# A decoder trunk on one core: operands of the feed-forward matmuls 64 and 96 bytes further in their buffers

## The chip, the cores and the metric

The kernel runs as one program on one core of a Trainium2 chip. The metric is the device time of one execution in microseconds (us). The profile names the engines PE (TensorE, matmuls), PEld (TensorE, loading of the stationary operand), DVE (VectorE), ACT (ScalarE), POOL (GpSimd) and SP (SyncE, which issues the DMAs here).

## What is computed

Two decoder layers over 256 tokens of width 1024, in float32: a dilated-attention mixer, then a mixer of forgetting attention, each followed by a SwiGLU feed-forward layer, and a last RMS norm.

```python
def swiglu(h, w_gu, w_down):          # h: 256 x 1024, D_FF = 2816
    gu = h @ w_gu
    g, u = gu[..., :D_FF], gu[..., D_FF:]
    return (jax.nn.silu(g) * u) @ w_down

def reference(x, ...):
    h = x
    for i in range(2):
        j = i // 2
        if i % 2 == 0:
            h = h + dilated_mixer(rmsnorm(h, a_norm[j]), a_w_in[j], a_w_out[j])
        else:
            h = h + forgetting_mixer(rmsnorm(h, b_norm[j]), b_w_in[j], b_f[j], b_w_out[j])
        h = h + swiglu(rmsnorm(h, ffn_norm[i]), ffn_w_gu[i], ffn_w_down[i])
    return rmsnorm(h, final_norm)
```

## The kernel before

**Split operands.** Nearly every product is made with numbers split in two: `split` (L76) writes the high part of a tile with ACT (L80, type float32r) and the rest with DVE (L84). `mm3` (L236) makes one product out of three matmuls: stationary high by moving high (L239), stationary high by moving low, stationary low by moving high (both L244). Each matmul loads its own stationary operand first, 128 columns of it, so there is one weight load to one matmul. The moving operand has 256 or 512 columns.

**The feed-forward layer** (`ffn`, called once for each layer). The 2816 columns are cut into 22 blocks of 128 (index f). For block f, `up` multiplies the weights (stationary, tiles `wh` and `wl`) by the normed activations (moving, tile `xt`, 256 tokens): 2 x 8 products, 48 matmuls of 256 columns. SiLU and the product with the other half follow on ACT and DVE, and the result is split into the tiles `ah` and `al` (`act`, L797). After every second block comes the down-projection of a pair of blocks (index j, 11 pairs), which adds into the output for two halves of 128 tokens and four column blocks of 256. It is done with one level of Strassen's scheme in Winograd's form for half of the columns:

- `down(j, t)`: for pairs j up to 8, columns 0 to 511 only, 6 matmuls of 512 columns for each half t of the tokens: stationary `ah`/`al`, moving `wh`/`wl`.
- `down_7(j)`: seven products of 256 columns, so 21 matmuls, in place of eight. Their stationary operands are `ah`/`al` or the sums of activation blocks `sh`/`sl`, which `combine` (L752) makes; their moving operands are `wh`/`wl` or the sums of weight blocks `th`/`tl`, which `sums_of` (L119) makes.

For j from 1 to 7 the order on TensorE is `up`, `up`, `down(j, 0)`, `down(j, 1)`, `down_7(j)`: 96 matmuls of 256 columns, 12 of 512, 21 of 256, without a pause. For j = 8, only `down(8, 0)` stands between two `up`; the rest of it comes in the tail of the layer with pairs 9 and 10, which are done in full. The weights of pair 8 lie in the tiles `oth`/`otl`.

**Where the operands lie.** Every tile has a place in each partition's row of SBUF, given by a pool with one ring of buffers to a tag. The buffers of a tag have the size of the largest tile under it, and the tags follow each other. Of the built program these are the places of the operands that the text speaks of, as the byte address of the first buffer, the step to the next buffer, and the remainder of every buffer's address by 128:

| Operand | Tag | First address | Step | Remainder by 128 |
|---|---|---|---|---|
| wh, wl (weights) | wh, wl | 8544, 43360 | 8704 | 96 |
| oth, otl (weights of pair 8) | oth, otl | 115040, 123232 | - | 96 |
| xt (normed activations, high and low part in turn) | xt | 131872 | 1024 | 32 |
| sh, sl (sums of activation blocks) | v | 156512 | 2048 | 96 |
| ah, al (gated activations) | p | 185184 | 2560 | 96 |
| th, tl (sums of weight blocks) | bias | 210048 | 3072 | 0 |

Inside a buffer the matmuls start at multiples of 512 bytes, except in one product of the second mixer (272 columns), whose weights step by 1088 bytes, and in fp32 matmuls of the attention, which the change does not touch. So the remainder of a buffer is that of every operand taken from it. The two that meet on TensorE at one time are the moving operand of a matmul and the stationary operand of the matmul behind it, which is loaded meanwhile. The text writes such a pair as moving/stationary: 32/96 for `up`, 96/96 and 0/96 for the down-projection. The mixers' projections with `xt` stationary are 96/32.

Of the kernel before, what the change touches and what calls it, by code (L numbers as in the profile page):

```python
# [11 lines left out]
F32R = mybir.dt.float32r  # L12
# [5 lines left out]
P = 128  # L18
# [14 lines left out]
def trunk(ctx: ExitStack, tc: tile.TileContext, T, out):  # L33
# [4 lines left out]
    ap = ctx.enter_context(tc.tile_pool(name="ap", bufs=1))  # L38
# [5 lines left out]
    def first():  # L44

        return tc.high_priority(offset=300)

    def psum(tag):
        return ps.tile([P, 512], F32, tag=tag, name=f"ps_{tag}", bufs=2)
# [26 lines left out]
    def split(pair, view, src, early=True, after=None, hold=None):  # L76
        hi, lo = pair
        with first() if early else nullcontext():
            with behind_(hold):
                a = nc.scalar.activation(view(hi), src, AF.Copy)  # L80

            def low(after=None):
                with tc.issue_after(after.ins) if after else nullcontext():
                    return nc.vector.tensor_tensor(view(lo), src, view(hi).bitcast(F32), op=ALU.subtract)  # L84

            if isinstance(after, list):
                return after.append(low)
            return a, low(after)


    def piece(key, todo=None):
        if key[0][:2] == "dn" and key[1] == LATE - 1:
            wh, wl = (y.rearrange("p k c -> p (k c)") for y in fm_tile("ot", KT, 1))
        else:
            wh, wl = (wp.tile([P, WIDE], F32R, tag=y, name=y, bufs=4) for y in ("wh", "wl"))
        if key == GATED:
            wh, wl = (y.rearrange("p (k c) -> p k c", k=KT) for y in (wh, wl))
        if key[0][:2] == "dn" and key[1] < LATE:
            todo += sums_of(key, (wh, wl))
            return wh, wl  # L100
        for c in range(2):
            raw = wp.tile([P, 1024], F32, tag="raw", name="raw", bufs=5)
            u = slice(c * 1024, (c + 1) * 1024)
            nc.sync.dma_start(raw, T[key[0]][key[1]][:, u])
            view = lambda y, u=u: y[:, u]
            if key == GATED:
                raw = raw.rearrange("p (k c) -> p k c", c=256)
                view = lambda y, c=c: y[:, c * 4:c * 4 + 4, :256]
            cut = lambda after=None, hold=None, raw=raw, view=view: split((wh, wl), view, raw, False, after, hold)
            if todo is None:  # L110
                cut()
            else:
                todo.append(cut)
        if key == GATED:
            cut = lambda after=None, hold=None: split((wh, wl), lambda y: y[:, :, 256:], wf32, False, after, hold)
            todo.append(cut)
        return wh, wl

    def sums_of(key, w):  # L119

        if key[1] == LATE - 1:
            raw = [wp.tile([P, 1024], F32, tag="raw", name="raw", bufs=5) for _ in range(2)]
        else:
            both_f = ap.tile([P, KT * S], F32, tag=("oth", "otl")[key[1] % 2], name="rawd", bufs=1)
            raw = [both_f[:, c * 1024:(c + 1) * 1024] for c in range(2)]
        for c in range(2):
            nc.sync.dma_start(raw[c], T[key[0]][key[1]][:, c * 1024:(c + 1) * 1024])
        b11, b12, b21, b22 = (raw[f][:, c:c + S] for f in range(2) for c in (512, 768))
        sums = ap.tile([P, 768], F32, tag="pt", name="ts", bufs=3)
        t3, t2, t4 = (sums[:, i * S:(i + 1) * S] for i in range(3))  # L130
        pair = tuple(ap.tile([P, 768], F32R, tag="bias", name=f"t{y}", bufs=4) for y in "hl")
        summed[key] = pair

        def plus(o, a, b):
            nc.vector.tensor_tensor(o, a, b, op=ALU.add)

        def cut(c, after=None, hold=None):
            if c == 0:
                plus(t3, b12, b22)
                plus(b12, b11, b12)  # L140
                plus(t2, b22, b12)
                plus(t4, t2, b21)
            elif c == 2:
                return split(pair, lambda y: y, sums, False, after, hold)
            return split(w, lambda y: y[:, c * 1024:(c + 1) * 1024], raw[c], False, after, hold)

        return [lambda after=None, hold=None, c=c: cut(c, after, hold) for c in range(3)]
# [141 lines left out]
    def p_tile(n=512, dtype=F32, name="p"):  # L289
        return ap.tile([P, 640], dtype, tag="p", name=name, bufs=6)[:, :n]  # L290
# [115 lines left out]
    def square(i):  # L406
        return nc.scalar.activation(part[i].rearrange("p (j s) -> p j s", s=S), xs[i], AF.Square, scale=D ** -0.5)
# [5 lines left out]
    for k in range(KT):  # L413
# [3 lines left out]
        with first(), in_order(cut):  # L417
            if k == 0:
                a = nc.vector.tensor_scalar(hi[:, k], xk[k], g, None, op0=ALU.mult)
            else:  # L420
                a = nc.scalar.activation(hi[:, k], xk[k], AF.Copy, scale=g)
# [4 lines left out]
        if k in (1, 5, 7):  # L426
            with first(), in_order(cut):
                a = [square(i) for i in {1: (0, 1), 5: (2,), 7: (3,)}[k]][-1]
# [12 lines left out]
    with first(), in_order(cut):  # L441
        a = square(4)
# [22 lines left out]
    x = []  # L465
# [133 lines left out]
    for i, (hq, g, w) in enumerate(a_units):  # L599
# [15 lines left out]
        if i in (24, 31):  # L615
            x.append(hrow("x"))
            t = len(x) - 1
            nc.sync.dma_start(x[t], T["x"][t * P:(t + 1) * P, :])
        if w < 2:
# [26 lines left out]
            if w == 1:  # L646

                j = i + (hq == 0)
# [92 lines left out]
    def ffn(l, hs, xt, grow, mid):  # L741
        acc = {}
        acts = {}
        rows_f = {}
        combos = {}
# [6 lines left out]
        def combine(j, a):  # L752

            y = ap.tile([P, 512], F32, tag="pt", name="sa4", bufs=3)
            b = a.rearrange("p (b c) -> p b c", c=P)
            z = y.rearrange("p (b c) -> p b c", c=P)
            with first():
                nc.vector.tensor_tensor(z[:, :2], b[:, 1:2].to_broadcast([P, 2, P]), b[:, 0:4:3], op=ALU.subtract)
                nc.vector.tensor_tensor(z[:, 2], z[:, 1], b[:, 0], op=ALU.subtract)
                nc.vector.tensor_tensor(z[:, 3], b[:, 2], z[:, 2], op=ALU.add)  # L760
            combos[j] = tuple(ap.tile([P, 512], F32R, tag="v", name=f"s{x}", bufs=7) for x in "hl")
            split(combos[j], lambda y: y, y)

        def down_7(j):
# [31 lines left out]

        def act(f):  # L797
            if f % 2 == 0:
                acts[f // 2] = tuple(p_tile(512, F32R, f"a{y}") for y in "hl")
            return acts[f // 2], lambda y: y[:, (f % 2) * S:(f % 2 + 1) * S]  # L800

        def gated(g, u, shape):
            sa = ap.tile([P, 512], F32, tag="qr", name="sa", bufs=3)
            sg, a = (sa[:, i * S:(i + 1) * S].rearrange("p (a b) -> p a b", a=shape) for i in range(2))
            with first():
                nc.scalar.activation(sg, g, AF.Silu)
                nc.vector.tensor_tensor(a, u, sg, op=ALU.mult)
            return a
# [6 lines left out]
        def up_with(f, wt):  # L815
            sg = ap.tile([P, 512], F32, tag="qr", name="sa", bufs=3)[:, :S]
            a = pair_of(f // 2)[:, f % 2 * S:(f % 2 + 1) * S]
            g, u = (psum("mm")[:, :S] for _ in range(2))
            proj_feat(xt, wt, g, 0)
            with first():  # L820
                nc.scalar.activation(sg, g, AF.Silu)  # L821
            proj_feat(xt, wt, u, 1)
            with first():
                nc.vector.tensor_tensor(a, u, sg, op=ALU.mult)  # L824
            split(*act(f), a)
            if f % 2 and 1 < f // 2 < LATE:
                combine(f // 2, rows_f.pop(f // 2))
# [32 lines left out]
        pair = [psum(("o", "mm")[l]) for _ in range(2)]  # L860
# [16 lines left out]
        for f in range(2):  # L877
            for t in range(2):
                nc.tensor.transpose(tr[:, f * S + t * P:f * S + (t + 1) * P], rows[t][:, f, :], ident)
        act(0)  # L880
        split(acts[0], lambda y: y, tr)
        nc.scalar.activation(pair_of(0), tr, AF.Copy)
        combine(0, rows_f.pop(0))
        third = act(2)
        up(3)
        gu = o.rearrange("p (a c b) -> p a c b", a=2, c=2)
        a = gated(gu[:, :, 0, :], gu[:, :, 1, :], 2)
# [3 lines left out]
        split(*third, tr[:, :S])  # L891
        nc.scalar.activation(rows_f[1][:, :S], tr[:, :S], AF.Copy)
        combine(1, rows_f.pop(1))
        for f in range(2, NF):
            if f > 3:
                up(f)
            if f % 2 == 0:
                j = f // 2 - 1
# [178 lines left out]
    for i, (hq, w) in enumerate(b_units):  # L1077
# [5 lines left out]
        if w < 2:  # L1083
# [15 lines left out]
            if w == 1:  # L1099
                j = i + 1  # L1100
# [39 lines left out]
    for o, (a, b) in zip(acc, ((0, 512), (512, 256), (768, 256))):  # L1140
        s = slice(a, a + b)
# [8 lines left out]
    v = ap.tile([P, 2], F32, tag="rs", name="rs", bufs=4)  # L1150
# [10 lines left out]
    for n in range(2):  # L1161
        s = slice(n * 256, n * 256 + 256)
# [3 lines left out]
        s = slice(n * 256, 256 + n * 352)  # L1166
# [88 lines left out]
```

## Time and profile before

| | |
|---|---|
| Time, median of 3 runs | 732.5 us (732.27 to 734.28) |
| The profiled execution's own time | 732.42 us |
| Its span, first to last instruction | 730.6 us |
| Granted TensorE clock, mean | 0.997 |
| PE busy | 722.6 us, 5988 matmuls |
| PEld busy | 674.5 us, 5988 loads |
| DVE busy | 566.9 us |
| ACT busy | 416.9 us |
| DMA, share of 16 engines, queue q1 | 59.0% |

Between the span and the profiled execution's own time lie 1.8 us. The page lists groups of instructions by line; a matmul's duration there runs from its start until its last result, and neighbours overlap. What a matmul costs is the distance from its start to the next one's start, which the timeline shows.

### The profile page before, as it was taken

The page shows a single profiled execution, that of the slowest core. Times are in us where ns is not written, and L with a number is a line of the kernel's source. Part 1 is how long each engine was busy: PE and PEld are TensorE (multiplying, and loading weights), DVE is VectorE, ACT ScalarE, POOL GpSimd, SP SyncE. Part 2 cuts the span into 40 slices and gives each one's busy share as a digit, 9 for nine tenths or more (in the row PEclk, how much of TensorE's full clock was granted, in tenths as well). Part 3 has the DMA queues.
Part 4 walks back from the last instruction along what each step waited for, and adds up shares of the span by engine and source line. Part 5 has one row for each costly group of instructions (what it writes and reads, how often), then busy time and mean ns, then how long its engine had stood idle before and what let it go on. Part 6 is the DMA issues. An engine that isn't in the chain of part 4 may idle for free.

```text
span 730.6 us, 14753 instructions
## 1 busy us (share of the span) xinstructions
PE 722.6 (99%) x5988; PEld 674.5 (92%) x5988; DVE 566.9 (78%) x938; ACT 416.9 (57%) x659; POOL 83.5 (11%) x118
## 2 busy tenths in 40 slices
PE   9999999999999999999999999999999999999996
PEld 7999989999988899999999989999889999999995
DVE  6997998998996788877778484586878977777825
ACT  7646747648545656655546353587475655545621
POOL 0600206008105000000000014120010000000001
PEclk9999999999999999999999999999999999999998
DMA  9865856855864494766348442883548576534601
GB/s 335 309 203 174 225 180 187 278 198 146 269 196 159 124 334 163 255 209 210 121 130 266 141 156 88 297 267 130 172 148 342 175 239 213 182 127 146 219 1 59
DMA packets 55045, 141.97 MB, mean 194 GB/s; under 512 B 20257, under 2 KB 21441, under 8 KB 54977
## 3 DMA queue, kind: packets, MB, share of 16 engines
q1 hardware_dynamic: 54832, 140.81, 59.0%
q8 instruction: 47, 0.77, 0.4%
q10 hardware_dynamic: 144, 0.21, 0.1%
q14 instruction: 22, 0.17, 0.1%
HBM read 136.00 MB, written 1.07 MB: 188 GB/s over the span
## 4 chain that ended last, share of the span: by engine, by line
PE 96%; ACT 1%; DMA 1%; DVE 1%; issue 0%; SPq 0%; POOL 0%; POOLq 0%; DVEq 0%; ACTq 0%
PE ps_mm L244 44%; PE ps_mm L239 22%; PE ps_sc L244 7%; PE ps_o L244 6%; PE ps_sc L239 4%; PE ps_o L239 3%; PE ps_tr L244 2%; PE ps_o L350 2%; PE ps_tr L239 1%; DMA otl<-in_lead 1%; PE ps_sc L513 1%; PE ps_tr L232 1%; PE ps_tr L338 1%; PE ps_sc L1006 0%; PE ps_sc L495 0%; ACT wh L80 0%
## 5 line engine op out<-in xcount | busy, mean ns | idle before, releaser
L239 PE MATMUL ps_mm<-xt,wh 128*128 128x256 f32 x1120 | 311.5, 278 | 0.1
L244 PE MATMUL ps_mm<-xt,wl 128*128 128x256 f32 x1120 | 309.9, 277 | 0.1
L244 PE MATMUL ps_mm<-xt,wh 128*128 128x256 f32 x1120 | 309.7, 277 | 0.0
L80 ACT ACTIVATE wh<-raw 128x1024 fp32r<-128x1024 f32 x204 | 210.4, 1056 | 136.9 <-PE ps_mm L244 71.4
L84 DVE TENSOR_TENSOR wl<-raw,wh 128x1024 fp32r<-128x1024 f32 x204 | 248.5, 1242 | 28.6 <-ACT wh L80 28.6
L239 PEld LDWEIGHTS ps_mm<-xt,wh 128*128 128x128 f32 x1120 | 210.3, 188 | 3.2 <-issue 1.7
L244 PEld LDWEIGHTS ps_mm<-xt,wl 128*128 128x128 f32 x1120 | 210.6, 188 | 0.3 <-DVE wl L84 0.3
L244 PEld LDWEIGHTS ps_mm<-xt,wh 128*128 128x128 f32 x1120 | 210.4, 188 | 0.2
L824 DVE TENSOR_TENSOR a<-ps_mm,sa 128x256 f32<-128x256 f32 x38 | 16.0, 422 | 50.4 <-PE ps_mm L244 50.4
L209 POOL TENSOR_SCALAR rs<-ssq 128x1 f32<-128x1 f32 x7 | 2.7, 391 | 419.6 <-ACT junk L218 419.6
L80 ACT ACTIVATE wh<-rawd 128x1024 fp32r<-128x1024 f32 x32 | 33.6, 1056 | 28.5 <-PE ps_mm L244 22.6
L239 PE MATMUL ps_mm<-wh,xt 128*128 128x512 f32 (+1 forms) x144 | 49.8, 346 | 0.0
L244 PE MATMUL ps_mm<-wh,xt 128*128 128x512 f32 (+1 forms) x149 | 49.2, 335 | 0.0
L244 PE MATMUL ps_mm<-wl,xt 128*128 128x512 f32 (+1 forms) x149 | 49.1, 335 | 0.0
L322 POOL COPY v<-v 32x256 f32<-32x256 f32 x64 | 40.4, 631 | 69.4 <-ACT v L317 66.8
L84 DVE TENSOR_TENSOR wl<-rawd,wh 128x1024 fp32r<-128x1024 f32 x32 | 39.0, 1225 | 1.7 <-ACT wh L80 1.6
L244 PEld LDWEIGHTS ps_mm<-wl,xt 128*128 128x128 f32 x149 | 28.0, 188 | 3.1
L244 PEld LDWEIGHTS ps_mm<-wh,xt 128*128 128x128 f32 x149 | 27.6, 188 | 3.3 <-DVE xt L84 0.3
L239 PEld LDWEIGHTS ps_mm<-wh,xt 128*128 128x128 f32 x144 | 27.0, 188 | 3.5 <-issue 0.3
L569 ACT COPY pt<-turned 128x1280 uint16<-128x1280 uint16 x12 | 19.4, 1671 | 13.9 <-DMA turned<-pt 13.9
L821 ACT ACTIVATE sa<-ps_mm 128x256 f32<-128x256 f32 x38 | 14.6, 383 | 21.2 <-PE ps_mm L244 20.6
L566 POOL COPY pt<-p 128x1280 uint16<-128x1280 uint16 x12 | 16.6, 1404 | 79.8 <-DVE p L546 38.8
(297 smaller groups left out, 1207.7 us busy)
## 6 DMA issues: line engine op xcount, KB each, us to landing
raw<-in_gu SPq DMA_DIRECT2D x88, 512.0 KB, 5.0
raw<-in_a_in SPq DMA_DIRECT2D x68, 512.0 KB, 4.9
rawd<-in_dn SPq DMA_DIRECT2D x32, 512.0 KB, 4.8
raw<-in_b_in SPq DMA_DIRECT2D x24, 512.0 KB, 4.7
raw<-in_dn SPq DMA_DIRECT2D x12, 512.0 KB, 4.8
raw<-in_a_out SPq DMA_DIRECT2D x8, 512.0 KB, 5.2
raw<-in_b_out SPq DMA_DIRECT2D x8, 512.0 KB, 4.0
bias<-sums SPq DMA_DIRECT2D x8, 384.0 KB, 5.7
```

Source lines behind the costliest of these rows:

```text
L80: a = nc.scalar.activation(view(hi), src, AF.Copy)
L84: return nc.vector.tensor_tensor(view(lo), src, view(hi).bitcast(F32), op=ALU.subtract)
L232: nc.tensor.transpose(tr[:, k * P:(k + 1) * P], xn[:, kk * P:(kk + 1) * P], ident)
L239: nc.tensor.matmul(o, sh, mh, start=start, stop=False)
L244: last = nc.tensor.matmul(o[:, u], s, m[:, u], start=False, stop=end and u.stop == n)
L322: nc.gpsimd.tensor_copy(v[1 + a % 2][n:n + 32, a // 2 * S:a // 2 * S + S], by_t[a * 32:a * 32 + 32, t, g])
L338: nc.tensor.transpose(tr[:, i * P:(i + 1) * P], b, ident)
L350: nc.tensor.matmul(o[h * HD:(h + 1) * HD], v[:, c:c + HD], w(h), start=start, stop=stop)
L566: nc.gpsimd.tensor_copy(split16.rearrange("p (t c) -> p t c", t=2), parts(quad["pt"][pr, h]))
L569: nc.scalar.copy(parts(w), turned.rearrange("p (t c) -> p t c", t=2))
L821: nc.scalar.activation(sg, g, AF.Silu)
L824: nc.vector.tensor_tensor(a, u, sg, op=ALU.mult)
```

## The change

Three tiles are made wider, and the part that is used starts further in. `act`: the tile is 528 columns wide and the 512 from column 16 on are used (64 bytes). `combine`: 544 columns, used from column 16 (64 bytes). `sums_of`: 800 columns, 768 used from column 24 (96 bytes).

```diff
 def sums_of(key, w):
-        pair = tuple(ap.tile([P, 768], F32R, tag="bias", name=f"t{y}", bufs=4) for y in "hl")
+        pair = tuple(ap.tile([P, 800], F32R, tag="bias", name=f"t{y}", bufs=4)[:, 24:792] for y in "hl")
...
 def combine(j, a):
-            combos[j] = tuple(ap.tile([P, 512], F32R, tag="v", name=f"s{x}", bufs=7) for x in "hl")
+            combos[j] = tuple(ap.tile([P, 544], F32R, tag="v", name=f"s{x}", bufs=7)[:, 16:528] for x in "hl")
...
 def act(f):
-                acts[f // 2] = tuple(p_tile(512, F32R, f"a{y}") for y in "hl")
+                acts[f // 2] = tuple(p_tile(528, F32R, f"a{y}")[:, 16:] for y in "hl")
```

No instruction is added, taken away or moved on any engine, and no wait changes. The buffers of tag `p` stay as wide as they were (640 columns); those of tags `v` and `bias` grow by 128 bytes each, so whatever lies behind them moves by 896 or 1408 bytes, multiples of 128. The places after the change:

| Operand | First address used | Step | Remainder by 128 |
|---|---|---|---|
| sh, sl | 156576 | 2176 | 32 |
| ah, al | 186144 | 2560 | 32 |
| th, tl | 211040 | 3200 | 96 |
| all other operands | moved by 0, 896 or 1408 | as before | as before |

All matmuls of the down-projection become 96/32 pairs.

## The prediction

> **What bounds the kernel now.** The page comes first: the shares of the engines and the chain of work that ended last.
>
> ```profile
> span 730.6 us, 14753 instructions
> PE 722.6 (99%) x5988; PEld 674.5 (92%) x5988; DVE 566.9 (78%) x938; ACT 416.9 (57%) x659; POOL 83.5 (11%) x118
> ...
> PE 96%; ACT 1%; DMA 1%; DVE 1%; issue 0%; SPq 0%; POOL 0%; POOLq 0%; DVEq 0%; ACTq 0%
> ```
>
> TensorE sets the end: it is on 96% of the chain and nearly never idle. A busy engine can still be slowed from inside, so the next view is the timeline of TensorE, read by the distance between starts. Here is one block of layer 0: first and last of the 12 matmuls of 512 columns, then the first seven products of 21, then the first and last matmul of the two `up` (96 matmuls) and the start of the next block.
>
> ```profile
> 302.97 0.39 PE L239 MATMUL ps_sc<-wh,ah 128*128 128x512 f32 x1
> ...
> 305.48 0.39 PE L244 MATMUL ps_o<-wh,al 128*128 128x512 f32 x1
> 305.71 0.28 PE L239 MATMUL ps_tr<-wh,ah 128*128 128x256 f32 x1
> 305.82 0.28 PE L244 MATMUL ps_tr<-wl,ah 128*128 128x256 f32 x1
> 305.94 0.28 PE L244 MATMUL ps_tr<-wh,al 128*128 128x256 f32 x1
> 306.06 0.28 PE L239 MATMUL ps_tr<-th,sh 128*128 128x256 f32 x1
> 306.19 0.28 PE L244 MATMUL ps_tr<-tl,sh 128*128 128x256 f32 x1
> 306.30 0.28 PE L244 MATMUL ps_tr<-th,sl 128*128 128x256 f32 x1
> 306.42 0.28 PE L239 MATMUL ps_sc<-wh,ah 128*128 128x256 f32 x1
> ...
> 308.21 0.28 PE L239 MATMUL ps_mm<-xt,wh 128*128 128x256 f32 x1
> ...
> 308.56 0.28 PE L239 MATMUL ps_mm<-xt,wh 128*128 128x256 f32 x1
> ...
> 318.99 0.28 PE L244 MATMUL ps_mm<-xt,wl 128*128 128x256 f32 x1
> 319.10 0.39 PE L239 MATMUL ps_sc<-wh,ah 128*128 128x512 f32 x1
> ```
>
> No gap stands between them, yet equal matmuls do not cost the same. The windows view gives the lengths of the three stretches, and of a fourth that comes up below; the number ahead of the comma is the length.
>
> ```profile
> core 0: us, PE busy (x), PEclk, DMA share, GB/s
> 302.97:305.71 2.74, 2.74 (x15) 1.00 0.73 254
> 305.71:308.21 2.50, 2.50 (x23) 1.00 0.27 92
> 308.21:319.10 10.89, 10.89 (x98) 1.00 0.66 214
> 401.11:409.82 8.71, 8.71 (x75) 1.00 0.48 160
> ```
>
> By the counts of the code (the counts in brackets take in matmuls that end inside), 21 products took 2.50 us, 119.0 ns each; 96 matmuls of `up`, of the same shape and with the same one weight load each, took 10.89 us, 113.4 ns each; 12 of 512 columns took 2.74 us, 228.3 ns each. The granted clock is 1.00 in all of them. What differs, by the table of places, is the remainder of the operands' addresses: `up` is 32/96, a distance of 64 by 128; products with `wh` and `wl` are 96/96, and those with `th` and `tl` 0/96. The products with `th` and `tl` are the ones with the longest start distance (306.06 to 306.19).
>
> **The change, part by part.** It removes, adds and moves no instruction, no transfer and no wait; it makes all 96/96 and 0/96 pairs 96/32. So the sum is made of start distances on TensorE alone, and nothing can hide a gain or a loss there: the engine is the chain.
>
> First, what a 96/32 pair costs at 256 columns. The trace has it in the mixers, with `xt` stationary and weights moving. Two places show two rhythms, each right behind matmuls of 512 columns with the same pair.
>
> ```profile
> 217.36 0.39 PE L239 MATMUL ps_mm<-wh,xt 128*128 128x512 f32 x1
> 217.59 0.39 PE L244 MATMUL ps_mm<-wl,xt 128*128 128x512 f32 x1
> 217.81 0.39 PE L244 MATMUL ps_mm<-wh,xt 128*128 128x512 f32 x1
> 218.04 0.39 PE L239 MATMUL ps_mm<-wh,xt 128*128 128x512 f32 x1
> 218.28 0.39 PE L244 MATMUL ps_mm<-wl,xt 128*128 128x256 f32 x2
> ...
> 224.17 0.40 PE L239 MATMUL ps_sc<-wh,oth 128*128 128x512 f32 x1
> ```
>
> ```profile
> 113.61 0.39 PE L244 MATMUL ps_mm<-wh,xt 128*128 128x512 f32 x1
> 113.83 0.39 PE L239 MATMUL ps_mm<-wh,xt 128*128 128x512 f32 x1
> 114.06 0.40 PE L244 MATMUL ps_mm<-wl,xt 128*128 128x256 f32 x2
> 114.30 0.40 PE L244 MATMUL ps_mm<-wh,xt 128*128 128x256 f32 x2
> 114.54 0.28 PE L239 MATMUL ps_mm<-xt,wh 128*128 128x256 f32 x1
> ...
> 114.89 0.28 PE L239 MATMUL ps_mm<-xt,wh 128*128 128x256 f32 x1
> ```
>
> From 218.28 to 224.17 the 52 matmuls of 256 columns stand 113.3 ns apart: the fast rhythm. From 114.06 to 114.54 the four stand 0.12 us apart: the slow one, whose size the fourth row of the windows gives better: the 74 distances from 401.11 to 409.82, `up` right behind matmuls of 512 columns, are 117.7 ns each. So for a product the bounds are 113.4 and 117.7 ns against 119.0 now.
>
> Which rhythm comes seems to be set by the last matmul of 512 columns. At that shape a 96/32 pair makes distances that go in rotation, short, middle, long. The last one ahead of the fast rhythm is long (218.04 to 218.28, 0.24); the last one ahead of the slow rhythm is not (113.83 to 114.06, 0.23, behind 0.22). In the changed kernel the 12 matmuls come behind an `up` in the fast rhythm. The trace has one such start, in the mixer:
>
> ```profile
> 206.11 0.39 PE L239 MATMUL ps_mm<-wh,xt 128*128 128x512 f32 x1
> ...
> 207.94 0.39 PE L244 MATMUL ps_mm<-wh,xt 128*128 128x512 f32 x1
> 208.18 0.39 PE L239 MATMUL ps_mm<-wh,xt 128*128 128x512 f32 x1
> ```
>
> Its ninth distance is a long one (207.94 to 208.18, 0.24), the nine together 2.07 us or 230 ns each. Every third is long, so the twelfth would be, and the products behind it would be fast. I take 113.4 ns for them.
>
> Now the sum, in us for one block of j = 1 to 7. Products: 21 x (119.0 - 113.4) ns = 0.12 less. The first three matmuls of `up` behind them (308.21 to 308.56, 0.35) stand against 3 x 113.4 ns = 0.34: 0.01 less. The 12 of 512 columns at 230 against 228.3 ns: 0.02 more. Together 0.11 less. Pair 0 has the same 21 products, so there are 16 such blocks in two layers: 1.8 less.
>
> The tails. Each layer's tail has the 21 products of pair 8 and others of 256 columns, 73 in both layers by the code: 0.41 less if all get the fast rhythm, 0.1 if none does. Their phases I can't follow one by one; I take 0.25.
>
> The slow stretches of `up`. The one from 401.11 lasts until a pause. It comes behind the six matmuls of `down(8, 0)`, and layer 1 has the same place.
>
> ```profile
> 691.22 0.39 PE L244 MATMUL ps_sc<-oth,al 128*128 128x512 f32 x1
> 691.45 0.28 PE L239 MATMUL ps_mm<-xt,wh 128*128 128x256 f32 x1
> ...
> 700.16 0.28 PE L244 MATMUL ps_mm<-xt,wl 128*128 128x256 f32 x1
> ```
>
> There too 74 distances take 8.71 us (691.45 to 700.16). With the change six matmuls end on a long distance, the sixth in the rotation, so both stretches may turn fast: 75 x 4.3 ns = 0.32 each, 0.65 together. If only the matmuls' own pair counts, they stay: 0.
>
> DVE and ACT write the moved tiles with the same shapes as before. A price for writing at another place is not in the trace; it is bounded below by nothing and above by the idle time of these engines, 22% of DVE's time and 43% of ACT's, and neither is on the chain for more than 1%. I take nothing.
>
> Sum: 1.8 + 0.25 + 0.65 = 2.7 us less; the bounds of this case are 1.9 (tails 0.1, `up` stays slow) and 2.9. The profiled execution took 732.42 us, 0.08 below the median of the three runs; 732.42 - 2.7 = 729.7 us.
>
> **The rivals.** *Slow rhythm in the products.* If the phase is not as I read it, every product falls to 117.7 ns: 409 products by 1.3 ns make 0.5 less, the matmuls of 512 columns 0.3 more (16 x 0.02), and 732.2 us comes out. For it: of the two places shown, one is slow. Against it: the place with the right phase is fast.
>
> *The addresses have no part in it.* What costs could be that stationary operands here are activations freshly written, or that `down_7` goes from one output bank to the next. Then nothing changes: 732.4 us. Against it: the stretch from 401.11 is slow with weights stationary and `xt` moving, like the fast one from 308.21, and the 52 from 218.28 are fast with activations stationary. The Trainium skill's page "TensorE: Matmul & The Clock Gate" (section Step-by-step: what each phase is for) speaks for this rival: TensorE has two independent read ports of SBUF, so that loading the next weights takes no read bandwidth from the running matmul; by that rule the places of the two operands could not matter. The trace does not agree, as far as 119.0 against 113.4 ns for equal work shows.
>
> *Slow rhythm carried into `up`.* This is the one that ends slower. Now the blocks with `th` and `tl` stand ahead of `up`, and `up` is fast from its fourth matmul on. With 96/32 throughout, a slow rhythm could go on into the 96 matmuls of the next `up`: 96 x 4.3 ns = 0.41 us for each of 16 blocks, 6.6 us, less the 0.2 that slow products still leave: 738.8 us. It decides from about 7 blocks on (2.7 / 0.41). For it: from 401.11 and from 691.45 the slow rhythm did go on, for 74 matmuls. Against it: from 114.54 on, `up`-like matmuls (32/96) behind four slow ones (96/32) turn fast: the three from 114.54 to 114.89 take 0.35, like the three from 308.21. A swap of roles between the two remainders seems to end the slow rhythm.
>
> **How the numbers follow.** My forecast, products fast and `up` fast, has 0.66; slow products 0.16; no part of the addresses 0.08; slow `up` 0.10. A measurement of this kernel can tell about 0.3%, 2.2 us, from no change. The forecast's bounds, 1.9 and 2.9 less, lie on both sides of that: I give 0.54 of it to faster, with the stretches of `up` relieved, and 0.12 to no change. So faster 0.54, same 0.12 + 0.16 + 0.08 = 0.36, slower 0.10. The range goes from 728.9 to 732.6. Its low end is the far bound, 732.4 - 2.9 = 729.5, and 0.6 more, since the three runs of the kernel before lie 2.0 us apart and a median may miss by some tenths; its high end takes in the first two rivals. Slow `up` is left out.
>
> **What would show it.** Right: in the timeline of the changed kernel, the 21 products of a block take 2.38 us in place of 2.50, the 12 of 512 columns 2.75, `up` 10.88, and the 74 distances behind `down(8, 0)` 8.39. The mean durations of matmuls from `ah` and `sh` fall as the start distances do. Wrong: products at 117.7 ns (2.47 us a block) mean the first rival; 119.0 unchanged the second; `up` at 11.3 us a pair of blocks the third. A span that shrinks with these distances unchanged would mean that I have looked at the wrong thing altogether.

## The result, and the profile after

The changed kernel takes 736.9 us (median of 6 runs, 736.4 to 738.1), the kernel before on the same chip 733.2 (6 runs, 732.3 to 734.3): ratio 1.0053, 95% interval 1.0040 to 1.0066. It is slower by 3.8 us of the medians, and the forecast of 729.7 us with its range to 732.6 was wrong. The two profiled executions, which the rest of this text compares, took 737.0 and 732.4, 4.6 us apart. The page of the changed kernel, shares of the engines and of the chain:

```profile
span 735.2 us, 14753 instructions
PE 726.9 (99%) x5988; PEld 677.8 (92%) x5988; DVE 566.9 (77%) x938; ACT 415.7 (57%) x659; POOL 83.1 (11%) x118
...
PE 95%; ACT 2%; DMA 1%; DVE 1%; issue 1%; SPq 0%; POOL 0%; POOLq 0%; DVEq 0%; ACTq 0%
```

The same 5988 matmuls keep TensorE busy for 4.3 us longer (726.9 against 722.6), and the span is 4.6 us longer; no other engine is on the chain for more than 2%. The page can't say which matmuls. Both traces have the same matmuls in the same order, so the distance from each start to the next can be subtracted, one by one:

| Stretch of the kernel before (us of its span) | After minus before, us |
|---|---|
| start, 0 to 62 | +0.28 |
| first mixer, 113 to 141 and 168 to 196 | +1.04 and +1.04 |
| rest of the first mixer, up to 273 | +0.12 |
| first feed-forward layer, 273 to 433 | +1.22 |
| second mixer, 433 to 556 | +0.08 |
| second feed-forward layer, 556 to the end | +0.82 |

Nearly half of the loss lies in the first mixer, where the change edits no line. Its start, in the timeline of the changed kernel, at the place that the prediction showed of before:

```profile
113.87 0.39 PE L244 MATMUL ps_mm<-wh,xt 128*128 128x512 f32 x1
114.10 0.39 PE L239 MATMUL ps_mm<-wh,xt 128*128 128x512 f32 x1
114.33 0.39 PE L244 MATMUL ps_mm<-wl,xt 128*128 128x256 f32 x2
114.56 0.39 PE L244 MATMUL ps_mm<-wh,xt 128*128 128x256 f32 x2
114.79 0.28 PE L239 MATMUL ps_mm<-xt,wh 128*128 128x256 f32 x1
```

The 240 matmuls behind the last row, 239 distances, in the windows view, of the changed kernel and then of the kernel before:

```profile
114.79:142.94 28.15, 28.15 (x242) 1.00 0.76 230
```

```profile
114.54:141.63 27.09, 27.09 (x241) 1.00 0.79 231
```

Same clock, no gap, 117.8 against 113.3 ns each: before, four matmuls (96/32) in the slow rhythm (0.48 us from 114.06 to 114.54) led to 239 distances (32/96) in the fast rhythm; after, four in the fast one (their starts, 114.33 to 114.79, stand 113 or 114 ns apart) lead to 239 distances of 117.8 ns. The run at 168 does the same.

Now the block of two `up`. The windows of the changed kernel: 12 matmuls of 512 columns, 21 products, the 96 matmuls of `up` behind them; then the `up` two blocks later; then the stretch behind `down(8, 0)`.

```profile
core 0: us, PE busy (x), PEclk, DMA share, GB/s
289.51:292.25 2.74, 2.74 (x14) 1.00 0.86 305
292.25:294.72 2.47, 2.47 (x23) 1.00 0.80 209
294.72:306.02 11.30, 11.30 (x98) 1.00 0.83 299
327.81:338.71 10.90, 10.90 (x99) 1.00 0.66 214
404.97:413.37 8.40, 8.40 (x75) 1.00 0.52 175
```

The products went from 2.50 to 2.47 us, 117.6 ns each, not to the 2.38 that was forecast. One `up` is slow (11.30, 117.7 ns), another fast (10.90). The stretch behind `down(8, 0)` became fast, 8.40 against 8.71 us for 74 distances. But it ends at a pause, and 43 distances behind the pause, first of before and then of the changed kernel, went the other way:

```profile
410.51:415.40 4.89, 4.89 (x44) 1.00 0.61 209
```

```profile
414.08:419.15 5.07, 5.07 (x45) 1.00 0.60 207
```

In both layers together, the `up` behind pairs 1, 2 and 6 of the first and pairs 1 and 5 of the second are slow, and the half block behind pair 0 of the second. How the products begin, in the timeline:

```profile
292.02 0.39 PE L244 MATMUL ps_o<-wh,al 128*128 128x512 f32 x1
292.25 0.28 PE L239 MATMUL ps_tr<-wh,ah 128*128 128x256 f32 x1
292.37 0.28 PE L244 MATMUL ps_tr<-wl,ah 128*128 128x256 f32 x1
292.48 0.28 PE L244 MATMUL ps_tr<-wh,al 128*128 128x256 f32 x1
292.60 0.28 PE L239 MATMUL ps_tr<-th,sh 128*128 128x256 f32 x1
292.71 0.28 PE L244 MATMUL ps_tr<-tl,sh 128*128 128x256 f32 x1
```

The distance of 0.13 us between the two products with `th` (306.06 to 306.19 before) is gone (292.60 to 292.71), but they are not at 113.4 ns. Unrounded, the first three starts, those with `wh`, `wl` and `ah`, `al`, stand 113, 114 and 113 ns apart, which is the fast rhythm; from the first product with `th` and `sh` on it is 117 or 118. The matmul of 512 columns ahead, the twelfth, is a long one (232 ns).

Summed over both feed-forward layers, from the same subtraction: `up` +1.96 us (5.5 slow blocks of 0.41 make 2.3; two stretches of -0.30 and what lies behind their pauses make -0.3), products -0.64, matmuls of 512 columns with those on their borders +0.47, all others +0.17; together 1.96. The table's rows, which begin a little elsewhere, have 2.04.

### The profile page after: what moved, and what is told of

Same layout as the page of the kernel before. It is cut to its first block, busy times and chain, and to the rows that moved or that the text cites. A ratio compares the mean times of both kernels' runs of the same rounds, so it can differ in the third digit from the quotient of the medians.

```text
span 735.2 us, 14753 instructions
## 1 busy us (share of the span) xinstructions
PE 726.9 (99%) x5988; PEld 677.8 (92%) x5988; DVE 566.9 (77%) x938; ACT 415.7 (57%) x659; POOL 83.1 (11%) x118
## 4 chain that ended last, share of the span: by engine, by line
PE 95%; ACT 2%; DMA 1%; DVE 1%; issue 1%; SPq 0%; POOL 0%; POOLq 0%; DVEq 0%; ACTq 0%
PE ps_mm L244 44%; PE ps_mm L239 22%; PE ps_sc L244 7%; PE ps_o L244 6%; PE ps_sc L239 3%; PE ps_o L239 3%; PE ps_tr L244 2%; PE ps_o L350 2%; PE ps_tr L239 1%; DMA otl<-in_lead 1%; PE ps_sc L513 1%; PE ps_tr L232 1%; ACT wh L80 1%; PE ps_tr L338 1%; PE ps_sc L1006 0%
```

## The experiments

A word on names: an operand's remainder by 512 is its address modulo 512 bytes. A run's numbers of one stage are differences of start distances against the kernel before, as in the table.

**The kernel before, again, and the change, again**, for what two executions differ by.

> The kernel before once more, for a second trace of it. If the rhythm of TensorE in a stretch (113.3 or 117.7 ns from start to start at 256 columns) follows from the program alone, this trace shows the same stretches slow as the first one: 74 distances of 117.7 ns behind down(8, 0) in both layers, and both long runs of the first mixer that follow a projection of values (some 237 matmuls each, near 114 and 169 us) fast. If the first mixer's rhythm changes from execution to execution, one or both of these runs are slow here, each for 1.05 us.

> The changed kernel once more, for a second trace. If the rhythms follow from the program, the same stretches are slow: two long runs in the first mixer, one run in the second, and up behind pairs 1, 2 and 6 in the first layer and 0, 1 and 5 in the second. If they change from execution to execution, others are.

Measured 732.2 and 736.8 us. Each repeats its first trace stage by stage: the second trace of before lies 0.19 us below the first in sum, with every rhythm of a long stretch the same, and the second of the change has the same +1.04 twice in the first mixer, +0.43 and +0.42 in the same blocks. Only short stretches near the start of a layer differ. So a rhythm here is set by the program in the main, not by chance (with two exceptions, below).

**Wider buffers alone.** The tiles are as wide as in the change, but the part used starts at column 0.

```diff
+ap.tile([P, 800], F32R, tag="bias", name=f"t{y}", bufs=4)[:, :768]
+ap.tile([P, 544], F32R, tag="v", name=f"s{x}", bufs=7)[:, :512]
```

> The wider buffers alone: tiles of 544 and 800 columns, used from column 0, so that all pairs of the feed-forward layers stay 96/96 and 0/96 and only the buffers behind them move, by 896 or 1408 bytes. Theory of the carried rhythm (the pairs of the feed-forward layers matter, and what follows takes over their rhythm): the feed-forward layers as before, 733.2 us, no change. Theory of the moved buffers (the 2.1 us lost in the first mixer come from the other tiles' new places): the first mixer has two slow runs as in the changed kernel, 735.2 us. Theory of scatter: the two runs are slow in some executions and not in others, whatever the kernel; the times spread over 2 us.

Measured 738.7 us, ratio 1.0070 (1.0053 to 1.0087): slower than the whole change. The first mixer loses the same 2.08 us, seven blocks have a slow `up`, and the products take 117.5 to 119 ns. Padding by itself costs 0.7%; the offsets, on top of it, give 1.7 parts in 1000 back, about 1.2 us of this kernel, though the two intervals overlap.

**Activations alone.** Only the line in `act`.

```diff
+acts[f // 2] = tuple(p_tile(528, F32R, f"a{y}")[:, 16:] for y in "hl")
```

> Only the gated activations start 64 bytes further in; no buffer grows, nothing else moves. Their pairs with the weights become 96/32, with the sums of weights 0/32; the sums of activations stay 96/96 and 0/96. Carried rhythm: the last product ahead of up is still a 0/96 pair, so every up is fast from its fourth matmul on; the products of the activations (9 of 21) gain up to 5.6 ns each, 1 us in all at most; between 732.2 and 733.2 us. Moved buffers: as nothing else moves, the first mixer is as before; also 732.2 to 733.2. If the first mixer is slow here, moved buffers are not its cause.

Measured 734.1 us, 1.0009 (0.9999 to 1.0019). The first mixer is as before, all `up` are fast, but the products stay slow. The windows, 21 products and the `up` behind:

```profile
290.13:292.62 2.49, 2.49 (x22) 1.00 0.89 298
292.62:303.52 10.90, 10.90 (x99) 1.00 0.85 281
```

118.6 ns each, though those of `ah`, `al` with `wh`, `wl` are now 96/32; that the rest isn't seems to spoil them. A block is 0.05 us longer than before.

**The change without the sums of weight blocks.** The lines of `combine` and `act`, not that of `sums_of`, so that `th`, `tl` stay at 0 and their pairs are 0/32.

```diff
+combos[j] = tuple(ap.tile([P, 544], F32R, tag="v", name=f"s{x}", bufs=7)[:, 16:528] for x in "hl")
+acts[f // 2] = tuple(p_tile(528, F32R, f"a{y}")[:, 16:] for y in "hl")
```

> The change without its third part: activations and sums of activations at remainder 32, sums of weights left at 0. The last product ahead of up is a 0/32 pair. Carried rhythm: a pair that is not 64 apart ends what was carried, so up is fast in all blocks, and the 2.0 us that the changed kernel lost in up are not lost; the products with weights (12 of 21) gain some 2 to 5 ns: 732 to 733 us if the first mixer is fast, 734 to 735 if its two runs are slow. If up is slow in a third of the blocks as in the changed kernel, the third part has no share in it: 736 us and more.

Measured 736.1 us, 1.0037 (1.0025 to 1.0048). The first mixer again +2.08, `up` slow in four blocks, products 2.44 to 2.48 us a block. With the ring of `bias` as it was, the wider ring `v` is enough for the first mixer's loss.

**Nothing but a move.** An unused strip of 896 bytes behind ring `v`; no operand of the feed-forward layers changes its remainder by 128.

```diff
+ap.tile([P, 224], F32, tag="gv2", name="gv2", bufs=1)
```

> The kernel before with an empty strip of 896 bytes behind the ring of tag v: no ring grows, no operand starts further in, only the buffers behind the strip move, as far as in the changed kernel; the remainders by 128 stay, those by 512 change (352 to 224). Theory of the moved buffers: both long runs of the first mixer are slow, 1.04 us each, and the first run of up-like matmuls in the second mixer 0.5 us; 735.5 us or more. Theory of the ring step (values and sums in buffers that no longer step by 2048 bytes): as before, 733.0 us.

Measured 735.8 us, 1.0039 (1.0027 to 1.0052). The run of 239 distances in the first mixer:

```profile
114.27:142.42 28.15, 28.15 (x241) 1.00 0.76 226
```

Slow, as in the change, and the run at 168 too: +2.08 of the 3.5 us by which its trace is longer; the second mixer adds 0.77, the 16 blocks 0.04 each. All `up` between the products of one pair and the next stay fast. A move by a multiple of 128 that is none of 512 is not free.

**The ring of sums 128 bytes wider, and all behind it moved by 1024.** The tile of tag `v` is 544 columns, used from 0, and a strip of 128 bytes follows.

```diff
+ap.tile([P, 544], F32R, tag="v", name=f"s{x}", bufs=7)[:, :512]
+ap.tile([P, 32], F32, tag="gv2", name="gv2", bufs=1)
```

> The kernel before with the buffers of tag v 128 bytes wider (step 2176, used from column 0) and an empty strip of 128 bytes behind them, so that all other buffers move by 1024 bytes and keep their remainder by 512. Moved buffers: both long runs of the first mixer fast as before; what is lost is lost in the feed-forward layers alone, where the sums of activations lie at four remainders by 512: 0.4 us for each up that comes out slow. Ring step: the first mixer loses its 2.1 us here, 735 us or more.

Measured 732.7 us, 0.9996 (0.9987 to 1.0005): no change. Run of the first mixer:

```profile
115.70:142.80 27.10, 27.10 (x241) 1.00 0.78 228
```

**The change, with the rest where it was by 512.** The change, a strip of 128 bytes that makes the first move 1024, and an unused constant of 512 bytes (`gap`) taken out so that all fits.

```diff
+ap.tile([P, 32], F32, tag="gv2", name="gv2", bufs=1)
-cst.tile([P, P], F32, name="gap")
```

> The whole change, with the same strip of 128 bytes, and an unused tile of 512 bytes taken out of the constants to make room: the tags behind the ring keep their remainder by 512, but the rings of sums still step by 2176 and 3200 bytes. Moved buffers: first mixer fast, 2.1 us less than the changed kernel, 734.8 us or below by what up gains. Ring step: the first mixer stays slow, 736.9 us.

Measured 734.9 us, 1.0024 (1.0013 to 1.0035): 2 us less than the change. The first mixer is back to its time before (run of 239 distances 27.10 us). The stretches behind `down(8, 0)` gain 0.30 each, and what follows their pauses stays fast. What is left is `up`, slow behind pairs 0, 6 and 7 of the first layer and 5, 6 and 7 of the second, and the matmuls of 512 columns, 0.05 us a block longer than before; the products are still at 2.43 to 2.48 us.

**Which tile it is in the mixer.** Only the first mixer's tiles of rotated queries and keys (tags `fm0`, `fm1`, L475) move by 384 bytes, between two strips that keep all the rest in place by 512.

```diff
+ap.tile([P, 96], F32, tag="gf1", name="gf1", bufs=1)
+ap.tile([P, 32], F32, tag="gf2", name="gf2", bufs=1)
```

> The kernel before with the attention's queries and keys (tags fm0, fm1) alone moved by 384 bytes, the same remainder by 512 as in the changed kernel (224 in place of 352); all else keeps its remainder by 512. If the place of queries and keys sets the phase with which the first mixer's projections start behind the scores, both long runs of that mixer are slow: 2.1 us more, 735.0 us. If it is another moved buffer (softmax tiles, their transposes, the rotation's scratch), the mixers are as before: 733.0 us.

Measured 735.0 us, 1.0028 (1.0019 to 1.0037), but its profiled execution was the one of ten that took 732.6, and its run was fast:

```profile
114.31:141.41 27.10, 27.10 (x242) 1.00 0.80 233
```

So it was run once more.

> e9 once more, for a second trace: nine of its ten executions took about 735.0 us, the profiled one 732.6 with both long runs of the first mixer fast. If queries and keys set the phase, a trace of a 735 us execution has both runs slow (1.04 us each) and nothing else changed. If the 2.1 us lie elsewhere, both runs are fast in it.

Measured 735.3 us, and this time both runs are slow, +1.04 and +1.04, with nothing else in the first mixer (and +0.26 in the second):

```profile
114.52 0.39 PE L244 MATMUL ps_mm<-wh,xt 128*128 128x256 f32 x2
114.75 0.28 PE L239 MATMUL ps_mm<-xt,wh 128*128 128x256 f32 x1
...
142.90 0.28 PE L244 MATMUL ps_mm<-xt,wl 128*128 128x256 f32 x1
```

Queries and keys are operands of 128 small fp32 matmuls (L513, from 107.50 in before), some microseconds ahead of the run. Their place changes the start of a run of float32r matmuls that do not read them. With these places, one execution of eleven went the other way; that the nine without a trace lost the same is inferred from their times, 734.5 to 736.1 us.

**All remainders by 512 the same.** Strips around the rings of `v` and `bias` keep their steps multiples of 512, so that every stationary operand of the down-projection is at 416 and every moving one at 352: a distance of -64 by 512 (a 96/32 pair by 128, as in the change).

```diff
+ap.tile([P, 16], F32, tag="gv1", name="gv1", bufs=1)
+ap.tile([P, 112], F32, tag="gv2", name="gv2", bufs=1)
+ap.tile([P, 56], F32, tag="gb1", name="gb1", bufs=1)
+ap.tile([P, 72], F32, tag="gb2", name="gb2", bufs=1)
+acts[f // 2] = tuple(p_tile(528, F32R, f"a{y}")[:, 16:] for y in "hl")
-cst.tile([P, P], F32, name="gap")
```

> No ring grows. Strips of 64 and 448 bytes around the ring of tag v and of 224 and 288 bytes around that of tag bias, the unused tile of 512 bytes out, activations 64 bytes further in: by 512, all stationary operands of the down-projection lie at 416, all moving ones at 352, as in up they lie at 352 and 288; the distance is -64 in all of them. Carried rhythm by 512: no distance changes from the products to up, so nothing flips; products at 113.4 ns and fast up, 2.5 to 3 us less than before, 730 to 730.5 us, if the 12 matmuls ahead end on the right phase; else products and up both slow in those blocks, and 735 us or more. The attention's values and bias tiles move by 64 and 224 bytes here, which may cost or gain in the mixers: read stage by stage.

Measured 737.5 us, 1.0060 (1.0044 to 1.0076). The windows, 12 of 512 columns, 21 products, and an `up`:

```profile
287.73:290.53 2.80, 2.80 (x14) 1.00 1.04 325
290.53:292.92 2.39, 2.39 (x23) 1.00 0.88 279
309.42:320.73 11.31, 11.31 (x98) 1.00 0.63 212
```

Here are the products as forecast: 113.8 ns, in every block. And behind every one of them `up` is slow, 117.8 ns, so that a block is 0.37 us longer. This is what the rival to which the prediction gave 0.10 forecast, `up` slow in every block, but here it stands behind products in the fast rhythm.

**+64 in place of -64.** The same with the strips of `v` exchanged and the activations 112 columns in: stationary at 288, moving at 352.

> The same places as e12 in the order of the kernel before (down_7 last). Carried rhythm: fast products lead to a slow up through the swap of roles, and a slow up starts the 512 columns on another phase, so blocks with fast products and slow up come in turn with others: 733 to 736 us, and no block in which products and up are both fast. If e12 is fast and this one too, the order is of no account.

Measured 734.5 us, 1.0027 (1.0015 to 1.0039); the profiled execution took 738.2, 2.5 us of it in the first 62 us, where no product of a feed-forward layer lies. Two blocks that follow each other, products and `up` of each:

```profile
292.33:294.81 2.48, 2.48 (x23) 1.00 0.93 282
294.81:305.70 10.89, 10.89 (x99) 1.00 0.86 291
308.45:310.83 2.38, 2.38 (x23) 1.00 0.14 41
310.83:322.14 11.31, 11.31 (x99) 1.00 0.67 213
```

Slow products, fast `up`; fast products, slow `up`; in strict turn. At the border the roles swap: the products have moving operands at 96 by 128 and stationary ones at 32, `up` the reverse. The rhythm is not carried over the border, it flips.

**Another order.** If the swap flips, a stretch of 512 columns between products and `up` may change what it meets. The places of -64, with `down_7(j)` ahead of `down(j, 1)` for pairs 1 to 7:

```diff
-                    down(j, 1)
-                    down_7(j)
+                    if j:
+                        down_7(j)
+                        down(j, 1)
```

> As e8 (all operands of the down-projection at a distance of -64 by 512), and for pairs 1 to 7 down_7 stands ahead of the second down, so that up follows matmuls of 512 columns and not the fast products. Carried rhythm with a swap of roles: six matmuls of 512 columns at this distance end on a long one and lead to a fast up, as behind down(8, 0) in e8; products fast too. In each of 14 blocks up gains 0.37 us against e8: 5.2 us less than e8, 732.3, or some 0.5 to 2.5 us below the kernel before if the start of the program goes as there (730.5 to 732.5 us). If up stays slow behind fast products whatever stands between, 737 us as e8.

Measured 735.0 us, 1.0035 (1.0022 to 1.0049). Products and `up` of two blocks in a row:

```profile
288.61:291.00 2.39, 2.39 (x23) 1.00 0.70 214
292.39:303.29 10.90, 10.90 (x97) 1.00 0.82 296
304.68:307.16 2.48, 2.48 (x23) 1.00 0.64 192
308.55:319.86 11.31, 11.31 (x98) 1.00 0.66 212
```

Fast with fast, then slow with slow. With six matmuls of 512 columns ahead of the products and six ahead of `up`, both go together.

**+64 and the other order.** The places of +64, with `down_7(j)` ahead of `down(j, 1)` for pairs 1 to 7.

> As e10, with all stationary operands of the down-projection at 288 by 512 in place of 416, so at a distance of +64 from the moving ones, as the mixers' projections with xt stationary have it; the second down behind down_7. Carried rhythm: behind a fast up six matmuls of 512 columns go short, middle, long, short, middle, long, and what follows a long one is fast, products and up alike (in the changed kernel up behind down(8, 0) did so): 16 blocks with products at 113.4 ns and fast up, 0.10 us less each, and both stretches behind down(8, 0) fast: 2 to 2.5 us below the kernel before, 730.5 us. If the distance's sign is of no account, fast and slow blocks alternate as in e10: 735 us.

Measured 730.9 us (11 runs, 730.3 to 732.8), ratio 0.9974 (0.9965 to 0.9983): by the median 2.0 us faster than the kernel before. A block of its trace, six of 512 columns, products, `up`:

```profile
303.84:305.21 1.37, 1.37 (x8) 1.00 0.79 254
305.21:307.59 2.38, 2.38 (x22) 1.00 0.59 200
308.96:319.87 10.91, 10.91 (x97) 1.00 0.67 214
```

Products at 113.3 ns and `up` at 113.6. From 303.84 to 319.87 a block takes 16.03 us, before 16.13 (302.97 to 319.10). Two blocks' products and the 48 matmuls of `up` behind pair 0 are slow in each layer. But the profiled execution was the slowest of the eleven, 732.75 us, and its span, 730.9 us, is 0.3 longer than that of before. So the trace shows the rhythms of the blocks, not the 2.0 us; where the other executions gain the rest is not shown. The `up` behind the last of these blocks in the second layer turned slow in its middle, behind one long distance (684.74 to 684.92), with no change of places there, and took 11.19 us in all:

```profile
684.51 0.28 PE L244 MATMUL ps_mm<-xt,wh 128*128 128x256 f32 x1
684.62 0.28 PE L244 MATMUL ps_mm<-xt,wl 128*128 128x256 f32 x1
684.74 0.35 PE L239 MATMUL ps_mm<-xt,wh 128*128 128x256 f32 x1
684.92 0.28 PE L244 MATMUL ps_mm<-xt,wh 128*128 128x256 f32 x1
685.04 0.28 PE L244 MATMUL ps_mm<-xt,wl 128*128 128x256 f32 x1
```

## Why the prediction was wrong

The forecast was 2.7 us less; the profiled execution is 4.6 longer. Of these 7.3 us some 2.1 lie in the first mixer, 2.3 in slow `up`, 1.5 in products (16 x 0.12 and 0.25 were forecast, 0.64 came) and 0.3 at `down(8, 0)`; no other term is above 0.3.

*"Whatever lies behind them moves by 896 or 1408 bytes, multiples of 128"*, as the section on the change has it, was taken as nothing: in the prediction the change "makes all 96/96 and 0/96 pairs 96/32", and no rival stood for the rest. This is the first step that failed: 2.1 us of the 4.6. A move alone costs it (2.08 with the strip of 896 bytes), undoing the move by 512 takes it away (the change with the rest in place), and the tiles of queries and keys alone bring it (+1.04 twice). The table of places gave remainders by 128, and the rule that "the remainder of a buffer is that of every operand" was right for 128 and too coarse. Every move of these tiles was by an odd multiple of 128 or by a multiple of 512, so whether 256 would do isn't told apart. The step from place to loss is the one that the prediction had seen at 114.54: before, four matmuls in the slow rhythm lead to 239 distances in the fast one; after the move it is the other way round.

*Products fast, 113.4 ns, 1.8 us less and 0.25 in the tails.* They came to 117.4 ns in the mean, -0.6 us. The price of a fast product was right: 113.3 to 113.8 ns in the fast blocks where all places agree by 512 (-64 or +64). What was wrong is that a 96/32 pair by 128 is enough. In the change the steps of the rings, 2176 and 3200 bytes, put `sh`, `sl`, `th` and `tl` at four remainders by 512 (416, 32, 160, 288 and 96, 224, 352, 480; the weights stay at 352), so within 21 products the distances change between plus and minus 64 and 192. `ah` and `al` lie at 288, +64 from the weights in all buffers, and with them the first three products behind a fast `up` do stand 113 or 114 ns apart; the sums end it, in all eight such blocks of pairs 1 to 7, within the next two products, with distances of 117 to 119 ns. That the mixed distances are what ends it is inferred from this and from the kernels in which they agree; no run had agreeing places of -64 or +64 for one ring of sums only.

*"Every third is long, so the twelfth would be, and the products behind it would be fast."* This held as far as it went. In the changed kernel, behind a fast `up`, the twelfth is long (231 or 232 ns) and the first three products are fast, in eight blocks of eight. It failed where it was taken for all 21, and where `up` is slow: behind a slow `up` the 12 end otherwise (2.76 to 2.80 us against 2.75) and no block begins with three fast products. At +64 throughout, where the mixer row that it was read from also lies (288 and 352 by 512), it holds for all 21, in turn with slow blocks. At -64 it is turned round: with the activations alone moved, where `ah` and `al` lie at 416, the first three products behind a fast `up` are slow (117 to 119 ns), and with all at -64 those behind a slow `up` are fast from the second on. So the rule needs the sign of the distance by 512, which the table of remainders by 128 does not give.

*The rival "slow rhythm carried into `up`"* was the nearest: 5.5 blocks of 0.41 us, 2.3 in all, where it was priced at 0.41 a block and said to decide from about 7. Its chance, 0.10, looks low with this, and the mechanism was turned round: it isn't the slow products whose rhythm goes on. With all places the same by 512 and the order of before, products at 113 ns put `up` in the slow rhythm, and products at 118 ns in the fast one; with the change's mixed places, products of 116 to 118 ns in the mean lead to either, and which place makes which block slow is not shown. "A swap of roles between the two remainders seems to end the slow rhythm", the argument against it, saw one side of this. The other side would have said that fast products put `up` in the slow rhythm, 0.42 us lost a block for 0.12 gained. In the kernel before, slow products go with a fast `up`; that they protect it is inferred.

*The stretches behind `down(8, 0)`*: forecast to turn fast, 0.65 together; they did, by 0.30 each. What failed is that the text stopped at the pause: the matmuls behind it, fast before, turned slow (5.07 for 4.89 us; in the second layer 0.18 too), so that 0.3 of the 0.6 is left. The step took the pause for the end of the effect. *Matmuls of 512 columns*: 0.02 a block more, 0.3 us, was about right; 0.47 came, with the tails and the borders. *DVE and ACT*: nothing, as taken; their busy times are 566.9 and 415.7 against 566.9 and 416.9 us.

*"The addresses have no part in it"* is ruled out by the strip of 896 bytes, which changes nothing else, and for the products by the 113.3 to 113.8 ns to which strips and starts alone bring them. The page "TensorE: Matmul & The Clock Gate" of the Trainium skill (section Step-by-step: what each phase is for) says that loading the next weights takes no read bandwidth from the running matmul. What the prediction inferred from it, that the places could not matter, does not agree with 113.3 against 117.8 ns for equal matmuls at a clock of 1.00. Whether reading is what collides stays open: the runs show that places decide, not through what.

What else stays open: why the swap of roles flips the rhythm, why a +64 distance behaves otherwise than -64, and why the place of queries and keys sets the phase of the run behind them.

## What to carry to other kernels

On a TensorE-bound kernel the place of a buffer is part of the schedule: after any change that makes a tile wider or adds one, look at the start distances of the longest equal stretches, those of code that wasn't touched first. When operands are placed, settle all of them by a remainder that the runs bear out (512 here; 256 was not tried) and keep the ring steps multiples of it, then read what the stretch *behind* the improved one does. A stretch of 21 that gets faster is a loss if the 96 behind it get slower.

## What was not expected of the hardware

- A matmul of 256 columns with its own weight load has two steady start distances at a clock of 1.00, 113.3 and 117.8 ns, and mostly keeps one of them for as long as the places stay: 239 distances in one run. One distance of 0.18 us inside a stretch was seen to turn it.
- Which one is mostly decided at the entry of the stretch. Where all places agree by 512, it flips at a swap of the two remainders: 2.38 us of products lead to 11.31 of `up`, 2.48 to 10.89. Behind a pause it can be the other one, as in the change (8.40, then 5.07 us) and before (8.71, then 4.89), but need not be: in the change with the rest in place both sides are fast.
- Moving tiles by 384 bytes that only the fp32 matmuls ahead of it read makes each of two runs 1.04 us longer in one traced execution and neither in the other; by their times, ten executions of eleven lose it.
